# The second layer's expert stage: 32 more tokens gather the rows they chose, on four partitions each, and 352 instead of 384 go through all experts

## The chip, the cores and the metric

One core of a Trainium2 chip runs the whole program. The metric is device microseconds (us) from launch to the end, the median of several runs. TensorE (PE), VectorE (DVE), ScalarE (ACT), GpSimd (POOL) and SyncE (SP) work side by side. SP, ACT and POOL issue DMAs, which all run on the same 16 DMA engines.

## The reference

Two layers of a diffusion backbone over 512 latent tokens and 256 context tokens of width 1024. Each layer is a token mixer and then an expert stage, `peer_ffn`. In the second layer only the 512 latent tokens go through the expert stage. Of 16384 experts (128 x 128) every token chooses 128 (8 heads x 16), and its output is a weighted sum over these:

```python
q = (xb @ wq).reshape(T, 8, 2, 128)
s = einsum('thcq,hckq->thck', q, keys)
sv, si = top_k(s, 16)                       # per half of the key
top_s, top_j = top_k(sv[:,:,0,:,None] + sv[:,:,1,None,:], 16)
eidx = take(si[0]*128 + si[1], top_j)       # 128 experts of a token
gate = softmax(top_s)
act = gelu(einsum('td,thkd->thk', xb, u_tab[eidx]))
out = einsum('thk,thkd->td', gate * act, v_tab[eidx])
```

## The kernel before

`peer(l, xin)` is the expert stage of layer `l`. It treats its tokens in two ways at once.

**Dense tokens** (the first `Wd`: 512 of 768 in layer 0, 384 of 512 in layer 1) go through all 16384 experts, 128 of them at a time. `s_part(j)` loads 128 rows of U (`d.ur`, three buffers), splits them into a rounded part and a rest on ACT and DVE (`d.uh`, `d.ul`), and multiplies them with the activations in 24 matmuls (8 slices of the width x 3 products of the parts) whose moving side has `Wd` columns. ACT applies gelu and ACT's queue writes the result to DRAM (`Ad`). In the second loop over j ("V loop", `for j in range(NE)`) SP loads `Ad[j]`, 128 rows of V (`rt.vr`) and, every fourth j, a block of gates (`rt.gt` from `Gd`). DVE multiplies activation and gate (`rt.gm`), ACT and DVE split both V and the product, and PE adds 24 matmuls of `Wd` columns into eight PSUM banks.

The gates are built in between: `route` turns the scores of a tile of 128 tokens into expert numbers and gates on DVE. `build` takes `128 // GB` = 4 blocks of 32 tokens; a block makes one-hot tables on DVE, 64 fp16 matmuls on PE, and one 2 MB write to `Gd` from ACT's queue. `s_ahead(n)` puts n `s_part`s ahead of a route or a block, in layer 1 six before a route (twelve before the first) and three before a block. What is left of the 128 is done one by one in `trailing`.

**Gathered tokens** (the last 128 in layer 1, 256 in layer 0) sit one on each partition. For each of a token's 128 experts an indirect DMA of POOL (line 1524) fetches one row of U per partition into `grow` (128 x 1024 fp32, six buffers in layer 1, four in layer 0), and DVE takes the dot product with the token's row (line 1497). After gelu and gate, 128 more DMAs fetch rows of V, which DVE adds up (line 244, `tok`). `choose(n, after)` uses the gathers of two calls before, copies n indices (`at`) on DVE and issues n gathers. In layer 1 it is called with 3 twice per block, with 1 per `trailing` step, and in the V loop with `(NS - done) // max(1, CHE - j)`, `NS` = 256 and `CHE` = 128.

At the end all gathered sums are transposed on PE and added to x. The instructions of one engine are laid out by a list scheduler ahead of time, so the parts of a route stand between other DVE work, and engines run their own list in order.

Names in rows: `d.S` is the PSUM tile of `s_part`, `O` that of the V loop, `pv` the split parts of V and product, `rt.k` PSUM of routes and builds; a name's prefix (`rt.`, `d.`, `mrg.`) says only in which section the tile was made.

Of the kernel before, what the change touches and what calls it, by code (L numbers as in the profile page):

```python
# [11 lines left out]
F32, F32R, U32, I32, U8 = dt.float32, dt.float32r, dt.uint32, dt.int32, dt.uint8  # L12
# [195 lines left out]
NG = (2, 1)  # L208
TOK = (2, 1)
# [7 lines left out]
def body(tc, I, out, dbg=None, stop=None):  # L217
# [17 lines left out]
    def tt(o, a, b, op):  # L235
        return V.tensor_tensor(o, a, b, op=op)
# [41 lines left out]
    with pool("keep") as kp, pool("scr", space=DRAM) as dp:  # L278
# [1134 lines left out]
        def peer(l, xin):  # L1413
# [6 lines left out]
            Wd = W - 128 * NG[l]  # L1420
            NB = Wd // GB
            NS = 256 * NG[l]
# [15 lines left out]
            with pool("pnrm", side=far) as np_:  # L1438
                h = norm_mod((hp, hg), np_, psS, x, l, 1, t0, "S", Wd if CUT[l] else None)
# [35 lines left out]
            def token_rows(t):  # L1475

                r = T(gp, [128, 8, 128], F32, "grow", GBUF[l])
                a, _, hi, lo = h[-1]
# [12 lines left out]
            gs, got, done = [], [], [0, 0]  # L1491

            def use(g, r):
                s, e = gs[r // 256], r % 128
                w = s["w"]
                if r % 256 < 128:
                    V.scalar_tensor_tensor(g, g, 1.0, s["h"], A.mult, A.mult, accum_out=w[:, e:e + 1])  # L1497
                    if e == 127:
                        act(w, w, AF.Gelu_apprx_tanh)
                        tt(w, w, s["gate"], A.mult)  # L1500
                elif e == 0:
                    s["y"] = T(gp, [128, 1024], F32, "tok", TOK[l])
                    ts(s["y"], g, w[:, 0:1])
                else:
                    stt(s["y"], g, w[:, e:e + 1], s["y"])

            def choose(n, after):
                n = min(n, 256 * len(gs) - done[0])
                with tc.issue_after(after.ins):
                    done[1] += 1  # L1510
                    while got and got[0][2] <= done[1] - LAG[l]:
                        use(*got.pop(0)[:2])
                    if n:
                        at = T(gp, [128, 8], I32, "at", 3)
                        i = 0
                        while i < n:
                            r = done[0] + i
                            m = min(n - i, 128 - r % 128)
                            V.tensor_copy(at[:, i:i + m], gs[r // 256]["ei"][:, r % 128:r % 128 + m])  # L1519
                            i += m  # L1520
                for i in range(n):
                    r = done[0]
                    g = T(gp, [128, 1024], F32, "grow", GBUF[l])
                    G.indirect_dma_start(out=g, out_offset=None,  # L1524
                                         in_=I["Ur"] if r % 256 < 128 else I["V"].rearrange("l j i d -> (l j i) d"),
                                         in_offset=bass.IndirectOffsetOnAxis(ap=at[:, i:i + 1], axis=0))
                    got.append((g, r, done[1]))
                    done[0] += 1
# [85 lines left out]
            def route_rows(p, t, io16):  # L1614
                ij, gate = route(p, t, io16)
                ef = T(p, [128, 128], F32, "gr", 2)
                fl = [ij[:, c].rearrange("p h k -> p (h k)") for c in range(2)]
                ts(ef, fl[1], float(NE), float(l * NE * NE))
                ei = T(gp, [128, 128], I32, "ei", NG[l])
                tt(ei, ef, fl[0], A.add)  # L1620
                gs.append(dict(ei=ei, gate=gate.rearrange("p h k -> p (h k)"), h=rows[NT - 1 - t],
                               w=T(gp, [128, 128], F32, "gw", NG[l]), at=t))

            ND = Wd // 128
# [22 lines left out]
            else:  # L1647
# [3 lines left out]
                rows = [token_rows(t) for t in range(NT - 1, ND - 1, -1)]  # L1651
            rq.release()
            with pool("rg", side=far) as p:
# [9 lines left out]
                def build(t, f):  # L1663
# [11 lines left out]
                    for b in range(128 // GB):  # L1675
# [31 lines left out]
                order += range(ND)  # L1707
                for t in order:
# [4 lines left out]
                    ij, _ = route(p, t, io16)  # L1713
                    build(t, [ij[:, c].rearrange("p h k -> p (h k)") for c in range(3)])
# [65 lines left out]
            for s in gs:  # L1780
                tk = slice(t0 + 128 * s["at"], t0 + 128 * s["at"] + 128)
                for a in range(0, 8, 4):
                    ps = pso[nu % 8].rearrange("p (k t) -> p k t", t=128)
# [58 lines left out]
```

## Time and profile before

| | us |
|---|---|
| median of 3 runs (4926.05 to 4934.66) | 4933.41 |
| the profiled execution | 4910.86 |
| its span in the trace | 4909.1 |
| PE busy | 4506.6 (92%) |
| DVE busy | 3626.7 (74%) |
| mean DMA rate over the span | 238 GB/s |

The profiled execution is 22.55 us under the median and its span leaves 1.76 us around it. A busy time is the union of an engine's instructions; matmuls overlap their neighbours, so their own durations are longer than the distance from one to the next. The DMA share is the mean busy share of the 16 engines. Layer 1's expert stage is roughly the last quarter of the span, from 3560 us on.

### The profile page before, as it was taken

Reading aid. Unit: us, or ns where it says so; the run is one execution under the profiler, and the core shown is the slowest. Engines: PE = TensorE matmul, PEld = TensorE weight load, DVE = VectorE, ACT = ScalarE, POOL = GpSimd, SP = SyncE. Lnnn points to the kernel's source line nnn. Section 1 sums busy time; section 2 is a strip of 40 time slices with the busy share of each in tenths; the row PEclk is TensorE's granted clock in tenths of the full one; section 3 lists DMA queues with packets and bytes.
Section 4 is the critical chain, followed back from the end, with each engine's and each line's share of the span. In section 5 each row is a group of like instructions: output and inputs, shape, how many; then the busy total and the mean of one; then the engine's idle time right before and its main releaser. Section 6 shows DMA issues by size and latency. Waiting matters only on the chain. (4 is left out here: it accounts for less than half of the span.)

```text
span 4909.1 us, 66824 instructions
## 1 busy us (share of the span) xinstructions
PE 4506.6 (92%) x24203; PEld 3782.9 (77%) x24203; DVE 3626.7 (74%) x7303; ACT 1686.9 (34%) x2548; POOL 1358.9 (28%) x1117
## 2 busy tenths in 40 slices
PE   7879898899999999799999887998899998999998
PEld 4659576688777888687788664767589898999997
DVE  5772667499889997688898677466589975577787
ACT  4352223443223333222222435222533333333333
POOL 1211101002344544234555221111002332223332
PEclk9989998899999999899999998999999999999999
DMA  5441624356788999999999544334327889988896
GB/s 181 162 136 64 204 93 122 136 174 226 250 303 300 332 335 340 315 358 355 367 383 378 176 152 131 105 129 129 130 83 244 285 307 330 300 290 323 324 333 245
DMA packets 521083, 1170.01 MB, mean 238 GB/s; under 512 B 68192, under 2 KB 250272, under 8 KB 516272
## 3 DMA queue, kind: packets, MB, share of 16 engines
q1 hardware_dynamic: 227440, 563.42, 32.9%
q0 software_dynamic: 134912, 484.06, 27.8%
q10 hardware_dynamic: 158400, 118.25, 7.5%
q8 instruction: 191, 3.13, 0.3%
q14 instruction: 140, 1.15, 0.1%
HBM read 992.95 MB, written 173.02 MB: 238 GB/s over the span
## 5 line engine op out<-in xcount | busy, mean ns | idle before, releaser
L254 PE MATMUL d.S<-mrg.hhi,d.ul 128*128 128x512 f32 (+1 forms) x2048 | 767.0, 375 | 71.7 <-DVE d.ul L251 63.0
L1524 POOL DMA_INDIRECT d.grow<-in_V_dram,d.at x369 | 572.0, 1550 | 709.5 <-DVE d.at L1519 570.8
L254 PE MATMUL d.S<-mrg.hlo,d.uh 128*128 128x512 f32 (+1 forms) x2048 | 756.8, 370 | 0.1
L254 PE MATMUL d.S<-mrg.hhi,d.uh 128*128 128x512 f32 (+1 forms) x2048 | 754.7, 369 | 0.0
L254 PE MATMUL rt.O<-rt.pv,rt.pv 128*128 128x512 f32 (+1 forms) x2580 | 556.5, 365 | 39.7 <-DVE rt.pv L251 38.9
L254 PEld LDWEIGHTS rt.O<-rt.pv,rt.pv 128*128 128x128 f32 x2580 | 466.8, 188 | 105.7 <-issue 46.5
L254 PEld LDWEIGHTS d.S<-mrg.hhi,d.ul 128*128 128x128 f32 x2048 | 395.4, 193 | 126.1 <-DVE d.ul L251 76.6
L247 ACT ACTIVATE d.pa<-d.S 128x512 f32<-128x512 f32 (+1 forms) x256 | 139.7, 546 | 861.4 <-PE d.S L254 817.7
L251 DVE TENSOR_TENSOR d.ul<-d.ur,d.uh 128x1024 fp32r<-128x1024 f32 x256 | 312.3, 1221 | 157.7 <-ACT d.uh L250 151.9
L254 PEld LDWEIGHTS d.S<-mrg.hlo,d.uh 128*128 128x128 f32 x2048 | 394.8, 193 | 39.5 <-DVE mrg.hlo L251 0.9
L254 PEld LDWEIGHTS d.S<-mrg.hhi,d.uh 128*128 128x128 f32 x2048 | 393.3, 192 | 41.4
L1524 POOL DMA_INDIRECT d.grow<-in_Ur_dram,d.at x233 | 306.5, 1315 | 425.5 <-DVE d.at L1519 320.0
L1524 POOL DMA_INDIRECT rt.grow<-in_Ur_dram,rt.at x151 | 215.9, 1430 | 612.7 <-DVE rt.at L1519 566.8
L250 ACT CAST rt.pv<-rt.vr 128x1024 fp32r<-128x1024 f32 x172 | 181.2, 1053 | 580.7 <-PE d.O L254 260.8
L1497 DVE SCALAR_TENSOR_TENSOR d.grow<-d.grow,rt.tok 128x1024 f32<-128x1024 f32 x233 | 281.8, 1222 | 101.3 <-DMA d.grow<-in_Ur_dram,d.at 100.0
L244 DVE SCALAR_TENSOR_TENSOR d.tok<-d.grow,rt.gw,d.tok 128x1024 f32<-128x1024 f32 x245 | 314.3, 1283 | 50.5 <-DMA d.grow<-in_V_dram,d.at 50.0
L254 PE MATMUL d.O<-rt.pv,rt.pv 128*128 128x512 f32 (+1 forms) x1548 | 338.0, 362 | 0.0
L254 PEld LDWEIGHTS d.O<-rt.pv,rt.pv 128*128 128x128 f32 x1548 | 281.4, 188 | 30.1
L254 PE MATMUL rt.O<-d.pv,d.pv 128*128 128x512 f32 (+1 forms) x1260 | 272.2, 365 | 7.6 <-DVE d.pv L251 7.2
L250 ACT CAST d.uh<-d.ur 128x1024 fp32r<-128x1024 f32 x256 | 266.6, 1042 | 27.9 <-issue 9.0
L254 PEld LDWEIGHTS rt.O<-d.pv,d.pv 128*128 128x128 f32 x1260 | 228.4, 189 | 40.0 <-issue 10.9
L254 PE MATMUL z.z<-hhi,z.wlo 128*128 128x512 f32 (+1 forms) x656 | 236.1, 360 | 23.0 <-POOL z.wlo L251 16.2
(619 smaller groups left out, 9173.7 us busy)
## 6 DMA issues: line engine op xcount, KB each, us to landing
d.ur<-in_U_dram SPq DMA_DIRECT2D x256, 512.0 KB
rt.vr<-in_V_dram SPq DMA_DIRECT2D x256, 512.0 KB
ada.adaw<-in_ada_w_dram POOLq DMA_DIRECT2D x80, 512.0 KB
mrg.Ad<-d.pa ACTq DMA_DIRECT2D x128, 256.0 KB
rt.gt<-mrg.Gd SPq DMA_DIRECT2D x32, 1024.0 KB
rt.ga<-mrg.Ad SPq DMA_DIRECT2D x128, 256.0 KB
mrg.Gd<-ro.x ACTq DMA_DIRECT2D x14, 2048.0 KB
mrg.Gd<-rt.gst ACTq DMA_DIRECT2D x14, 2048.0 KB
```

Of the source, the lines that this page charges most:

```text
L244: return V.scalar_tensor_tensor(o, a, s, b, op0=op0, op1=op1)
L247: return S.activation(o, i, f, bias=bias, scale=scale)
L250: S.copy(hi, src)
L251: return (eng or V).tensor_tensor(lo, src, hi.bitcast(F32), op=A.subtract)
L254: PE.matmul(ps, l, r, start=start, stop=stop)
L1497: V.scalar_tensor_tensor(g, g, 1.0, s["h"], A.mult, A.mult, accum_out=w[:, e:e + 1])
L1524: G.indirect_dma_start(out=g, out_offset=None, in_=I["Ur"] if r % 256 < 128 else I["V"].rearrange("l j i d -> (l j i) d"), in_offset=bass. ...
```

## The change

`QP = (0, 4)` switches it on in layer 1 only. 32 of the 384 dense tokens (the last quarter of dense tile 2) become gathered tokens. Each sits on four partitions, 32 of its 128 experts on each, so 32 gathers of U and 32 of V serve all four quarters together. `Wd` falls from 384 to 352 and `NB`, the blocks of gates, from 12 to 11; `NS` rises from 256 to 320. `choose` now takes its rows from a list `plan` in the order the groups were routed: 128 U and 128 V of the first group, then 32 U and 32 V of the second.

Tile 2 is routed and built first of the three dense tiles, with three blocks instead of four. `token_rows` is called once more, for tile 2; its result is written to DRAM (`some`). `route_some` computes the expert numbers and issues 12 DMAs on SP's queue that put numbers, gates and token rows onto the four partition groups. At the end 8 matmuls with 32 columns add the four partial sums and transpose them, and 8 DVE instructions of 32 columns add them to x. The knobs for how many gathers go where (`CHN`, `CHT`, `CHE`, `GBUF`, `LAG`) stay. Layer 0 computes as before.

```diff
+QP = (0, 4)
...
-            Wd = W - 128 * NG[l]
+            Wh = W - 128 * NG[l]
+            nq = 128 // QP[l] if QP[l] else 0
+            Wd = Wh - nq
             NB = Wd // GB
-            NS = 256 * NG[l]
+            NS = 256 * NG[l] + (256 // QP[l] if QP[l] else 0)
...
             def token_rows(t):
...
-                ht = T(gp, [128, 1024], F32, "tok", TOK[l])
+                ht = T(gp, [128, 1024], F32, "tok", TOK[l]) if t >= ND else T(gp, [128, 1024], F32, "grow", GBUF[l])
...
+            plan = []
+
+            def chosen(s):
+                gs.append(s)
+                plan.extend((s, i, e) for i in range(2) for e in range(s["n"]))
...
             def choose(n, after):
-                n = min(n, 256 * len(gs) - done[0])
+                n = min(n, len(plan) - done[0])
...
+            def route_some(p, ij):
+
+                n = QP[l]
+                ea = T(p, [128, 128], I32, "ea", 1)
+                numbers(p, ij, ea)
+                eq = T(gp, [128, nq], I32, "eq", 1)
+                gq = T(gp, [128, nq], F32, "gq", 1)
+                hq = T(gp, [128, 1024], F32, "tokq", 1)
+                gf = ij[:, 2].rearrange("p h k -> p (h k)")
+                m = 128 // n
+                for i in range(n):
+                    to, of = slice(nq * i, nq * i + nq), slice(m * i, m * i + m)
+                    SP.dma_start(eq[to], ea[128 - nq:, of])
+                    SP.dma_start(gq[to], gf[128 - nq:, of])
+                    SP.dma_start(hq[to], some[128 - nq:])
+                chosen(dict(ei=eq, gate=gq, h=hq, n=m, w=T(gp, [128, m], F32, "wq", 1), at=Wd, tag=("tokq", 1)))
...
                 rows = [token_rows(t) for t in range(NT - 1, ND - 1, -1)]
+                if nq:
+                    sm_ = token_rows(ND - 1)
+                    some = T(dp, [128, 1024], F32, "some%d" % l)
+                    SP.dma_start(some, sm_)
...
-                    for b in range(128 // GB):
+                    for b in range((Wd - 128 * t) // GB if t == ND - 1 else 128 // GB):
...
-                order += range(ND)
+                order += ([ND - 1] + list(range(ND - 1))) if nq else range(ND)
...
                     ij, _ = route(p, t, io16)
+                    if nq and t == ND - 1:
+                        route_some(p, ij)
...
+                if nt < 128:
+
+                    one = T(p, [128, nt], F32, "one")
+                    tt(one, ident[:, 0:nt], ident[:, nt:2 * nt], A.add)
+                    for i in range(2, QP[l]):
+                        tt(one, one, ident[:, nt * i:nt * i + nt], A.add)
...
-                        tr(ps[:, k - a], s["y"][:, 128 * k:128 * k + 128])
+                        if nt < 128:
+                            mm(ps[:, k - a], s["y"][:, 128 * k:128 * k + 128], one, True, True)
+                        else:
+                            tr(ps[:, k - a], s["y"][:, 128 * k:128 * k + 128])
```

## Rows read from the trace of the kernel before

**Rows 1.** Page, busy time, share of the span and instructions of each engine
```profile
PE 4506.6 (92%) x24203; PEld 3782.9 (77%) x24203; DVE 3626.7 (74%) x7303; ACT 1686.9 (34%) x2548; POOL 1358.9 (28%) x1117
```

**Rows 2.** Windows, layer 1's expert stage by stage: routes, builds, turn, trailing, V loop, end
```profile
core 0: us, PE busy (x) PEld busy (x) DVE busy (x) ACT busy (x) POOL busy (x), PEclk, DMA share, GB/s
3628.00:3740.00 112.00, 102.06 (x534) 95.41 (x533) 103.71 (x416) 40.93 (x60) 4.31 (x3) 0.95 0.35 114
3740.00:4050.00 310.00, 293.38 (x1866) 285.18 (x1865) 260.68 (x391) 122.41 (x195) 115.17 (x72) 0.96 0.90 305
4050.00:4083.00 33.00, 18.89 (x97) 18.25 (x96) 14.79 (x25) 8.69 (x13) 3.53 (x3) 0.84 0.94 338
4083.00:4329.00 246.00, 243.51 (x1391) 242.13 (x1390) 145.04 (x233) 83.16 (x118) 65.38 (x58) 0.99 0.89 305
4329.00:4883.00 554.00, 542.60 (x3052) 529.59 (x3052) 433.35 (x618) 184.21 (x251) 195.53 (x122) 1.00 0.87 316
...
4883.00:4909.00 26.00, 12.05 (x46) 6.72 (x44) 12.02 (x24) 8.81 (x12) 0.00 (x0) 0.79 0.21 81
```

**Rows 3.** Timeline, PE: start, us, line, names, shape; 23 steps of 256, then 8 of 384
```profile
2861.63 0.28 PE L254 MATMUL z.z<-hhi,z.wlo 128*128 128x256 f32 x1
...
2864.38 0.28 PE L254 MATMUL z.z<-hhi,z.whi 128*128 128x256 f32 x1
...
4249.79 0.33 PE L254 MATMUL d.S<-mrg.hhi,d.ul 128*128 128x384 f32 x1
...
4251.18 0.33 PE L254 MATMUL d.S<-mrg.hhi,d.uh 128*128 128x384 f32 x1
```

**Rows 4.** Waits, 4329 to 4872 (V loop): who waited for whom, us, times, longest
```profile
DVE rt.tok L244 <- DMA d.grow<-in_V_dram,d.at: 97.8, 79, 3.7
ACT rt.pv L250 <- DMA rt.vr<-in_V_dram: 73.2, 21, 5.1
...
ACT d.pv L250 <- DMA rt.vr<-in_V_dram: 44.5, 13, 5.6
```

**Rows 5.** DMA issues of the whole span: names, queue, count, KB each
```profile
rt.vr<-in_V_dram SPq DMA_DIRECT2D x256, 512.0 KB
...
mrg.Ad<-d.pa ACTq DMA_DIRECT2D x128, 192.0 KB
rt.gt<-mrg.Gd SPq DMA_DIRECT2D x32, 768.0 KB
rt.ga<-mrg.Ad SPq DMA_DIRECT2D x128, 192.0 KB
```

**Rows 6.** Windows, part of layer 0's V loop, then most of layer 1's
```profile
2400.00:2700.00 300.00, 298.99 (x1307) 244.31 (x1307) 270.17 (x325) 84.92 (x109) 160.35 (x109) 1.00 1.00 382
...
4450.00:4860.00 410.00, 399.62 (x2231) 387.21 (x2230) 322.57 (x463) 137.15 (x187) 154.43 (x93) 1.00 0.90 326
```

**Rows 7.** Groups on DVE: layer 0, 2400 to 2700; then layer 1, 4400 to 4850
```profile
L244 DVE SCALAR_TENSOR_TENSOR d.tok<-d.grow,rt.gw,d.tok 128x1024 f32<-128x1024 f32 x109 | 139.9, 1283 | 28.6 <-DMA d.grow<-in_V_dram,d.at 28.4
...
L236 DVE TENSOR_TENSOR rt.gm<-rt.ga,rt.gt 128x512 f32<-128x512 f32 x54 | 37.4, 692 | 1.9
...
L236 DVE TENSOR_TENSOR rt.gm<-rt.ga,rt.gt 128x384 f32<-128x384 f32 x101 | 56.4, 558 | 3.5
```

**Rows 8.** Timeline, the writes of one tile's four blocks on ACT's queue
```profile
3750.34 0.38 ACTq L1698 DMA_DIRECT2D mrg.Gd<-ro.x  x1
3770.58 0.38 ACTq L1698 DMA_DIRECT2D mrg.Gd<-rt.gst  x1
3793.85 0.38 ACTq L1698 DMA_DIRECT2D mrg.Gd<-ro.x  x1
3814.96 0.38 ACTq L1698 DMA_DIRECT2D mrg.Gd<-rt.gst  x1
```

**Rows 9.** Waits of SP's queue, 3740 to 4330
```profile
SPq L1762 <- DMA mrg.Gd<-rt.gst: 13.3, 1, 13.3
```

**Rows 10.** Timeline: SP's load of U, the transposes of a token tile
```profile
4029.79 0.33 SPq L1450 DMA_DIRECT2D d.ur<-in_U_dram  x1
...
3650.07 1.04 PE L264 MATMUL rt.k<-cst,rt.grow 128*128 128x128 f32 x8
```

**Rows 11.** Groups on PE, 3740 to 4050 (builds)
```profile
L254 PE MATMUL d.S<-mrg.hhi,d.ul 128*128 128x384 f32 x364 | 129.3, 355 | 8.1 <-DVE d.ul L251 8.1
...
L254 PE MATMUL rt.k<-rt.og,ro.x 128*128 128x128 f16 x768 | 97.1, 297 | 8.6 <-ACT rt.gst L247 5.3 <-ACT ro.x L247 3.3
```

**Rows 12.** Timeline, DVE: the last additions to x
```profile
4883.06 2.72 DVE L244 SCALAR_TENSOR_TENSOR ro.x<-rt.O,mods,ro.x 128x384 f32<-128x384 f32 x5 [2.08 <-PE rt.O L254]
...
4887.26 2.15 DVE L244 SCALAR_TENSOR_TENSOR ro.x<-rt.O,mods,ro.x 128x128 f32<-128x128 f32 x8
```

More of the change, by code (lines that the diff above doesn't have):

```diff
@@ L1438, in peer @@
             with pool("pnrm", side=far) as np_:
-                h = norm_mod((hp, hg), np_, psS, x, l, 1, t0, "S", Wd if CUT[l] else None)
+                h = norm_mod((hp, hg), np_, psS, x, l, 1, t0, "S", Wh if CUT[l] else None)
             hi, lo = h[0][2:]
@@ L1477, in token_rows @@
                 r = T(gp, [128, 8, 128], F32, "grow", GBUF[l])
-                a, _, hi, lo = h[-1]
+                a, _, hi, lo = h[-1] if t >= ND else h[0]
                 tk = slice(128 * t - a, 128 * t - a + 128)
                 tt(r, hi[:, :, tk].bitcast(F32), lo[:, :, tk].bitcast(F32), A.add)
-                ht = T(gp, [128, 1024], F32, "tok", TOK[l])
+                ht = T(gp, [128, 1024], F32, "tok", TOK[l]) if t >= ND else T(gp, [128, 1024], F32, "grow", GBUF[l])
                 for a in range(0, 8, 4):
@@ L1491, in peer @@
             gs, got, done = [], [], [0, 0]
+            plan = []
+            def chosen(s):
+                gs.append(s)
+                plan.extend((s, i, e) for i in range(2) for e in range(s["n"]))
             def use(g, r):
-                s, e = gs[r // 256], r % 128
+                s, second, e = plan[r]
                 w = s["w"]
-                if r % 256 < 128:
+                if not second:
                     V.scalar_tensor_tensor(g, g, 1.0, s["h"], A.mult, A.mult, accum_out=w[:, e:e + 1])
-                    if e == 127:
+                    if e == s["n"] - 1:
                         act(w, w, AF.Gelu_apprx_tanh)
@@ L1516, in choose @@
                         while i < n:
[L1517 to L1519 removed]
+                            s, _, e = plan[done[0] + i]
+                            m = min(n - i, s["n"] - e)
+                            V.tensor_copy(at[:, i:i + m], s["ei"][:, e:e + m])
                             i += m
@@ L1524, in choose @@
                     G.indirect_dma_start(out=g, out_offset=None,
-                                         in_=I["Ur"] if r % 256 < 128 else I["V"].rearrange("l j i d -> (l j i) d"),
+                                         in_=I["V"].rearrange("l j i d -> (l j i) d") if plan[r][1] else I["Ur"],
                                          in_offset=bass.IndirectOffsetOnAxis(ap=at[:, i:i + 1], axis=0))
@@ L1612, in route, with numbers @@
                 return ij, gate
-            def route_rows(p, t, io16):
-                ij, gate = route(p, t, io16)
+            def numbers(p, ij, ei):
                 ef = T(p, [128, 128], F32, "gr", 2)
@@ L1618, in route_rows @@
                 ts(ef, fl[1], float(NE), float(l * NE * NE))
+                tt(ei, ef, fl[0], A.add)
+            def route_rows(p, t, io16):
+                ij, gate = route(p, t, io16)
                 ei = T(gp, [128, 128], I32, "ei", NG[l])
[L1620 to L1624, printed above, removed]
+                numbers(p, ij, ei)
+                chosen(dict(ei=ei, gate=gate.rearrange("p h k -> p (h k)"), h=rows[NT - 1 - t], n=128,
+                            w=T(gp, [128, 128], F32, "gw", NG[l]), at=128 * t, tag=("tok", TOK[l])))
+            def route_some(p, ij):
[13 more added lines that the diff above has]
+                chosen(dict(ei=eq, gate=gq, h=hq, n=m, w=T(gp, [128, m], F32, "wq", 1), at=Wd, tag=("tokq", 1)))
+            ND = Wh // 128
             SP.dma_start(xs[:, :, t0:], x[:, :, t0:])
@@ L1780, in peer @@
             for s in gs:
-                tk = slice(t0 + 128 * s["at"], t0 + 128 * s["at"] + 128)
+                nt = 128 if s["n"] == 128 else nq
+                tk = slice(t0 + s["at"], t0 + s["at"] + nt)
+                if nt < 128:
[3 more added lines that the diff above has]
+                        tt(one, one, ident[:, nt * i:nt * i + nt], A.add)
                 for a in range(0, 8, 4):
-                    ps = pso[nu % 8].rearrange("p (k t) -> p k t", t=128)
+                    ps = pso[nu % 8][:, 0:4 * nt].rearrange("p (k t) -> p k t", t=nt)
                     nu += 1
                     for k in range(a, a + 4):
-                        tr(ps[:, k - a], s["y"][:, 128 * k:128 * k + 128])
+                        if nt < 128:
+                            mm(ps[:, k - a], s["y"][:, 128 * k:128 * k + 128], one, True, True)
+                        else:
+                            tr(ps[:, k - a], s["y"][:, 128 * k:128 * k + 128])
                     for k in range(a, a + 4):
```

2 lines of the change are left out of this document (1 added, 1 removed).

## Prediction

> **What bounds the kernel now.** I start with the page's busy times [rows 1]: PE leads with 92% of the span, but that is a mean over many stages, and only layer 1's expert stage changes. So the windows come next, stage by stage [rows 2]. The reader should see three regimes. In *trailing* (4083 to 4329) PE is busy 243.5 of 246 us and the DMA share is 0.89: PE is the bound. In the *builds* (3740 to 4050) PE has 293 of 310, DVE 261 and the DMAs 0.90: three resources close together. In the *V loop* (4329 to 4883) PE shows 543 of 554, but it is not quite the limit. The matmul pitch says so [rows 3]: eight steps of 384 columns take 1.39 us, 0.174 each, so the 24 of one expert row j need 4.17 us, while 554 / 128 is 4.33. The waits name what is late [rows 4]: DVE waits 79 times, 97.8 us, for a gather to land, and ACT 73.2 + 44.5 us for a load of V. The V loop is a PE loop that leans on the DMAs.
>
> **The traffic per j in the V loop.** From the issue sizes [rows 5]: V 512 KB, `Ad` 192 KB, a quarter of 768 KB of gates, and one gather of 128 x 1024 fp32, 512 KB: 1408 KB now. After the change `Ad` and the gates shrink by 1/12 to 176 KB each: 1376 KB with one gather, 1888 KB with two.
>
> **How the gathers are spread.** This is arithmetic on the code, and it decides the case. Before: 12 blocks x 6 = 72 gathers in the builds, 62 in trailing (66 of the 128 U steps are placed with routes and builds), 122 left: none for the first six j, then one per j. After: 11 x 6 = 66, then 65 in trailing (63 U steps are placed earlier), 189 left for 128 j. The integer division gives 1 per j up to j = 66 and 2 per j for the last 61. So all the new gathers, and more, pile up in the last half of the V loop.
>
> **The change part by part.** All of it is against the profiled execution.
>
> *Narrower matmuls.* The pitch is 2.75 / 23 = 0.1196 us at 256 columns and 0.174 at 384 [rows 3], 0.42 ns a column, so 352 columns give 0.160: 3.85 us per j and stage instead of 4.17, 0.325 saved. Over 256 such steps that is 83 us, if nothing else is late. The rest of the sum is how much of that survives.
>
> *Routes (3628 to 3740).* 427 `d.S` matmuls run here, 17.8 steps; DVE, with the routes, is busy 104 of 112, as much as PE [rows 2]. 17.8 x 0.325 = 5.8 is the most; I take -4, ends 0 and -6.
>
> *Builds.* Within one tile the blocks' writes are 20.2, 23.3 and 21.1 us apart [rows 8], so a block is worth 21.5 us, and one goes: -21.5. The other 45 or so U steps here (364 x 3 / 24 [rows 11]) less three would save 42.5 x 0.325 = 13.8 on PE, but the 64 fp16 matmuls per block (768 for 12) do not shrink, and neither do DVE's tables or the gathers per block. I take half, -6.5. Sum -28, ends -21 and -35. The order of tiles (2, 0, 1) costs nothing: the same work in another order; its cover is the six U steps before each route.
>
> *The turn (4050 to 4083).* PE is busy 19 of 33 while the last gate write and the reload of x drain. They stay: 0.
>
> *Trailing.* 62 steps at 4.17 become 65. The DMAs carry 512 + 512 + 176 = 1200 KB per step; over 3.85 us that is 319 GB/s, against 305 at a share of 0.89 now [rows 2], so about 0.93. I allow 3.9 us: 253.5 - 258.5 = -5. Ends -8 (3.85) and +12 (no narrowing gain at all, three steps more).
>
> *V loop, first 67 j (one gather).* PE wants 3.85. The DMAs deliver 326 GB/s now [rows 6], which gives 1409 KB (in thousands) / 326 = 4.32, no gain. Between these ends I take 4.2, nearer to the row of the same loop, since the gather and V waits of rows 4 don't get shorter with fewer columns.
>
> *V loop, last 61 j (two gathers).* No such stretch exists in layer 1, but layer 0's V loop is one [rows 6]: 109 gathers on 54 j [rows 7], two per j. There the DMA share is 1.00 at 382 GB/s, and a j takes 300 / 54.5 = 5.5 us, where PE at 512 columns needs just as long (299 of 300 busy). Here PE would need 3.85, and DVE's busy time, 270 / 54.5 = 4.96, less twice 0.692 - 0.525 for the narrower product and its split (0.558 at 384 columns, 0.525 at 352 by the same slope), is 4.6. The DMAs need 1933 KB / 382 = 5.06. So the DMAs are last, 5.06 at best; layer 0's 5.5 is the other end. I take 5.2, near the first, because layer 0's 5.5 is PE's own need there.
> Here a page of the Trainium skill speaks otherwise: "DMA: Bandwidth & Descriptors", section "Where 436 GB/s comes from", puts the fabric ceiling at 435 GB/s and the HBM share of a core at about 358. By the first a j would be an estimated 4.4 us, by the second 5.4. No 300 us here show more than 382, which is above the one and below the other.
>
> V loop: 67 x 4.2 + 61 x 5.2 = 598.6 against 554, +45. Ends: 67 x 3.85 + 61 x 5.06 = 566.6, +13; 67 x 4.33 + 61 x 5.5 = 625.6, +72.
>
> *Added steps.* The extra `token_rows` is 8 transposes, 1.04 us on PE [rows 10], two copies, an addition and one 512 KB write: +2, ends 0 and 3. `route_some` puts 12 DMAs on SP's queue, 0.33 us each by the load of U [rows 10], 4 us of issue, and they wait for tile 2's route on DVE. Queued behind them are the loads of U; for these waits ACT's `d.uh`, then `d.ul`, then PE. With three U buffers loaded ahead most is hidden; if the list scheduler puts them before the route has finished, SP stands as it does now for a gate write, 13.3 us [rows 9]. I take +4, ends 0 and 13. At the end, four gathers instead of two are still to be added after the last j, plus 8 small matmuls and 8 DVE instructions (8 of 128 columns take 2.15 us [rows 12]): +4, ends 0 and 6. The new group's DVE and POOL work in the middle is inside the 5.2.
>
> **Sum.** -4 - 28 + 0 - 5 + 45 + 2 + 4 + 4 = +18. On the profiled 4910.86 that is 4929. The median of the three runs is 22.55 us above the profiled one; I carry that over unchanged: 4933.4 + 18 = 4951, 0.36% slower. About 0.2%, 10 us, is what a measurement can tell from no change.
>
> **The rivals.**
> *The queue absorbs it (faster).* Layer 0 runs full queues without losing PE time. If the same holds here, the first 67 j run at PE's 3.85 and the others at 5.06, +13; with builds at -34, trailing -7, routes -5 and added steps +6 the sum is -27: 4906. For it: share 1.00 at 382 GB/s in rows 6. Against: at one gather per j layer 1 has only 0.90 of share and waits all the same [rows 4]. It decides whether the first 67 j fall below about 4.0 us.
> *The gather chain (slower still).* DVE adds a row two calls after its issue, and a V split stands behind that wait in DVE's list. Two gathers per call make the landing later. Then the first half stays at 4.33 and the second is at layer 0's 5.5: +72 in place of +45, 4978. For it: 97.8 us of such waits already [rows 4]. Against: in layer 0 DVE waits only 28.6 us in 300 with two gathers and four buffers [rows 7].
> *Narrowing is worth nothing on PE.* Weight loads are busy 242 of 246 us in trailing [rows 2]. If they set the pitch, U steps and the first half stay as they are: routes 0, builds -21, trailing +12, V loop 67 x 4.33 + 61 x 5.2, +53, added +10: +54, 4987. Against it: at 256 columns the same kind of matmul, each with its own 128 x 128 weights, starts every 0.12 us [rows 3], which a load of 0.17 could not follow. The Trainium skill, "Perfetto Trace Analysis", section "Identifying the Most-Contended Engine", takes the weight-load busy share as the measure of TensorE's headroom; the pitch at 256 columns disagrees with reading it so here.
>
> **How the numbers follow.** My forecast 0.47, the absorbing queue 0.20, the gather chain 0.20, weight loads 0.05, and 0.08 that gains and losses cancel near zero. The range from 4908 to 4988 takes in most of the first rival and all of the second, and the forecast's unknowns; about 2 in 10 stay outside. The forecast itself spreads by some 20 us, so it gives part of its chance to no change. Faster by over 0.2%: 0.22; within 0.2%: 0.22; slower: 0.56.
>
> **What would show it.** Right: in the windows of the changed kernel the trailing stage shows about 3.9 us per step; the V loop is about 600 us long, with two stretches, the first near 4.2 us per j, the second near 5.2 with a DMA share near 1.00, 370 to 385 GB/s, and PE well below 90%; and one block fewer, some 28 us, before the turn. Wrong: a second half at 4.6 or less (then the DMAs deliver over 420 GB/s), a first half under 4.0, or trailing still at 4.17. A new wait of SP over 10 us in the builds would show `route_some` dearer than I put it.

## The result and the profile after

The changed kernel takes 4963.91 us (4958.61 to 4973.0, five runs), the one before 4933.41 in the same comparison: a ratio of 1.0075, 95% interval 1.0057 to 1.0093, 0.75% slower. The forecast was 4951 with a range from 4908 to 4988. The direction and the largest term came out, and the size within a factor of two (18 us slower forecast, 30.5 measured); the terms of trailing and of the end didn't, and the reason given for the first half of the V loop was wrong.

The page of the changed kernel, busy times (answers rows 1):

```profile
PE 4461.7 (90%) x24163; PEld 3724.8 (75%) x24163; DVE 3679.7 (74%) x7413; ACT 1678.7 (34%) x2543; POOL 1452.2 (29%) x1181
```

PE has 45 us less to do than before and the kernel is still slower: PE's work is not what was saved or lost. The windows of the changed kernel, columns as in rows 2: routes, builds, most of trailing, V loop with one gather, V loop with two, end:

```profile
3542.00:3742.00 200.00, 192.63 (x1032) 169.31 (x1031) 179.54 (x799) 76.84 (x125) 6.58 (x2) 0.99 0.34 109
3742.00:4036.70 294.70, 258.18 (x1711) 250.87 (x1711) 248.81 (x405) 113.59 (x182) 109.16 (x66) 0.90 0.87 288
4090.00:4300.00 210.00, 202.88 (x1221) 197.20 (x1221) 123.91 (x202) 71.47 (x102) 73.37 (x50) 0.99 0.90 308
4325.00:4610.00 285.00, 264.99 (x1563) 254.69 (x1562) 221.71 (x323) 94.13 (x130) 107.15 (x66) 0.98 0.89 317
4610.00:4925.00 315.00, 265.12 (x1501) 254.87 (x1500) 273.06 (x399) 90.82 (x122) 164.43 (x122) 0.95 0.98 365
4925.00:4961.00 36.00, 14.76 (x45) 8.25 (x44) 16.91 (x34) 8.80 (x12) 0.00 (x0) 0.74 0.23 87
```

Compare with rows 2. The second half of the V loop is the new thing: DMA share 0.98 at 365 GB/s, PE 265 of 315 us. The line above it looks like the old V loop, but PE there is busy 93%, not 98%. In the builds PE fell to 258 of 295, with a mean granted clock of 0.90 (before 0.96; the clock's levels are 1.2 and 2.4 GHz).

So that stages of different kernels can be set side by side, they are cut at events of the timeline: the starts of the first `d.S` matmul, of the first and the last fp16 matmul of the builds and of the last `d.S`, the end of the last `O` matmul, the end of the span. (Some expectations below cut the builds at the start of the last unbroken row of fp16 matmuls, which comes 1 to 3 us earlier.) All stages in us:

| kernel | routes | builds | U rest | V loop | end | sum | first `d.S` at |
|---|---|---|---|---|---|---|---|
| before | 213.7 | 308.1 | 279.6 | 558.0 | 22.4 | 1381.9 | 3527.2 |
| before, a second trace | 214.0 | 306.0 | 279.6 | 560.2 | 22.5 | 1382.2 | 3539.9 |
| the change | 199.2 | 295.6 | 285.9 | 602.3 | 35.6 | 1418.6 | 3542.7 |
| narrow_only | 197.0 | 292.9 | 282.1 | 556.8 | 22.5 | 1351.3 | 3530.0 |
| gathers_only | 215.3 | 301.6 | 286.9 | 604.8 | 35.4 | 1444.0 | 3549.2 |
| block_less | 211.4 | 290.2 | 291.6 | 559.1 | 22.4 | 1374.7 | 3535.2 |
| order_only | 215.4 | 309.8 | 280.3 | 564.1 | 22.4 | 1392.0 | 3543.1 |
| lag3 | 201.6 | 291.8 | 286.3 | 543.6 | 37.0 | 1360.4 | 3542.0 |
| before_lag3 | 211.9 | 310.9 | 281.5 | 532.8 | 22.4 | 1359.4 | 3531.9 |
| even_lag3 | 201.4 | 298.9 | 284.8 | 527.6 | 31.7 | 1344.4 | 3538.4 |
| trail3 | 200.4 | 296.3 | 269.1 | 526.8 | 30.9 | 1323.6 | 3534.5 |

The change costs 36.7 us by this table, 30.5 by the medians. The spans differ by 52, but 15.5 of that lies ahead of the first `d.S`, where nothing was changed.

Who waits in the two halves of the V loop of the changed kernel (waits on DVE, ACT and PE: total us, times, longest; the first three lines are of 4325 to 4610, the others of 4610 to 4925):

```profile
DVE rt.tok L246 <- DMA d.grow<-in_V_dram,d.at: 60.9, 47, 3.8
ACT rt.pv L252 <- DMA rt.vr<-in_V_dram: 69.1, 20, 6.0
PE rt.O L256 <- DVE rt.pv L253: 15.6, 15, 2.3
...
DVE rt.tok L246 <- DMA d.grow<-in_V_dram,d.at: 20.7, 19, 3.2
DVE d.grow L1506 <- DMA d.grow<-in_Ur_dram,d.at: 15.9, 15, 2.9
ACT rt.pv L252 <- DMA rt.vr<-in_V_dram: 38.9, 17, 6.4
```

The old wait of rows 4 is still there in the first half: DVE waits for a gather 47 times in about 66 rounds.

### The profile page after: what moved, and what is told of

Same layout as the page of the kernel before. It is cut to its first block, busy times and chain, and to the rows that moved or that the text cites. A ratio compares the mean times of both kernels' runs of the same rounds, so it can differ in the third digit from the quotient of the medians.

```text
span 4961.3 us, 66925 instructions
## 1 busy us (share of the span) xinstructions
PE 4461.7 (90%) x24163; PEld 3724.8 (75%) x24163; DVE 3679.7 (74%) x7413; ACT 1678.7 (34%) x2543; POOL 1452.2 (29%) x1181
## 3 DMA queue, kind: packets, MB, share of 16 engines
q14 instruction: 142, 1.16, 0.1%
## 5 line engine op out<-in xcount | busy, mean ns | idle before, releaser
L256 PE MATMUL d.S<-mrg.hhi,d.ul 128*128 128x512 f32 (+1 forms) x2048 | 756.5, 369 | 76.5 <-DVE d.ul L253 67.5
L1533 POOL DMA_INDIRECT d.grow<-in_V_dram,d.at x404 | 611.8, 1514 | 638.3 <-DVE d.at L1528 480.3
L256 PE MATMUL d.S<-mrg.hlo,d.uh 128*128 128x512 f32 (+1 forms) x2048 | 744.6, 364 | 0.1
L256 PE MATMUL d.S<-mrg.hhi,d.uh 128*128 128x512 f32 (+1 forms) x2048 | 741.0, 362 | 0.0
L256 PE MATMUL rt.O<-rt.pv,rt.pv 128*128 128x512 f32 (+1 forms) x2580 | 560.2, 367 | 83.5 <-DVE rt.pv L253 70.0
L1533 POOL DMA_INDIRECT d.grow<-in_Ur_dram,d.at x265 | 338.0, 1276 | 478.0 <-DVE d.at L1528 367.0
L1533 POOL DMA_INDIRECT rt.grow<-in_Ur_dram,rt.at x151 | 237.4, 1572 | 592.1 <-DVE rt.at L1528 548.2
L256 PE MATMUL rt.O<-d.pv,d.pv 128*128 128x512 f32 (+1 forms) x1260 | 267.6, 361 | 23.4 <-DVE d.pv L253 16.9
```

The source lines that it names most:

```text
L256: PE.matmul(ps, l, r, start=start, stop=stop)
L1533: G.indirect_dma_start(out=g, out_offset=None, in_=I["V"].rearrange("l j i d -> (l j i) d") if plan[r][1] else I["Ur"], in_offset=bass.Ind ...
```

## Experiments

The comparisons of one group share their runs of the kernel before, so its median differs a little from group to group (4925.71, 4925.25, 4930.56).

### The two halves of the change, each alone

narrow_only, against the changed kernel:

```diff
-            NS = 256 * NG[l] + (256 // QP[l] if QP[l] else 0)
+            NS = 256 * NG[l]
...
-                if nq:
-                    sm_ = token_rows(ND - 1)
...
-                    if nq and t == ND - 1:
-                        route_some(p, ij)
```

> The changed kernel without the second group of gathered tokens: 352 dense tokens, 256 gathers as in the kernel before, and no expert output for 32 tokens. It is the narrowing alone. If the pitch of a matmul follows its columns (24 in 3.85 us instead of 4.17), trailing runs at 3.9 us a step and the V loop at about 4.2 us per j, 538 us in place of 558 before and 602 after; the end loses its 13 us again: about 4885 us, 1% faster than the kernel before. If the weight loads set the pitch, trailing and V loop stay at 4.17 and 4.33 and only the missing block is gained: about 4923.

Measured: 4895.11 us, ratio 0.9942 (0.9925 to 0.996), 30.6 us faster. But the V loop is 556.8, as long as at 384 columns, where 538 was expected. Its waits on DVE and ACT, 4302 to 4859:

```profile
4302.00:4859.00 557.00, 517.41 (x3079) 497.32 (x3078) 431.77 (x630) 181.72 (x251) 202.62 (x124) 0.99 0.86 311
...
DVE rt.tok L246 <- DMA d.grow<-in_V_dram,d.at: 112.7, 89, 3.8
ACT rt.pv L252 <- DMA rt.vr<-in_V_dram: 114.1, 31, 5.8
```

gathers_only, against the changed kernel:

```diff
-            Wd = Wh - nq
+            Wd = Wh
...
-                chosen(dict(ei=eq, gate=gq, h=hq, n=m, w=T(gp, [128, m], F32, "wq", 1), at=Wd, tag=("tokq", 1)))
+                chosen(dict(ei=eq, gate=gq, h=hq, n=m, w=T(gp, [128, m], F32, "wq", 1), at=Wh - nq, tag=("tokq", 1)))
```

> The changed kernel with 384 dense tokens and 12 blocks of gates, and the second group gathered on top (32 tokens get their expert output twice). It is the cost of the 64 gathers alone. If the DMAs are full in the last 61 j (1920 KB per j at 382 GB/s is 5.15 us), the V loop is 67 x 4.33 + 61 x 5.15 = 604 us against 558 before, and the end takes 13 us more: about 4990 us, 1.2% slower than before. If two gathers per j fit beside 24 matmuls of 384 columns (the loop stays near 4.4), it is the end alone: about 4950.

Measured: 4989.66, ratio 1.0123 (1.0106 to 1.014), 64 us slower. The halves add up: 64 - 30.6 = 33, the change within its interval. What the 32 tokens save as dense tokens lies outside the V loop; of the 62.1 us that they cost as gathered ones by the table, 46.8 lie in it and 13.0 in the end.

### Is it bytes or the spread: even and half_bytes

even spreads the 189 gathers over all 128 j:

```diff
+                if j == 0:
+                    left = NS - done[0], done[0]
+                share = left[1] + left[0] * (j + 1) // NE - done[0] if l else (NS - done[0]) // max(1, CHE - j)
-                choose(min(8, (NS - done[0]) // max(1, CHE - j)), ins)
+                choose(min(8, share), ins)
```

> The changed kernel with the 189 gathers of the V loop spread evenly, 1 or 2 per j by the running sum, in place of 1 per j for 67 j and 2 per j for 61. Nothing else changes. If the loss comes from full DMAs in the second half alone, a j carries 1620 KB, 4.34 us at 382 GB/s, and the V loop falls from 602 to between 560 and 580: some 30 us faster than the changed kernel, about 4933. If every gather costs its share wherever it stands (4.2 with one, 5.2 with two, 4.7 in the mean), the loop stays at 602 and the time at 4964.

Measured: 5045.15, ratio 1.0251 (1.0227 to 1.0276): far slower, where both expectations had it no slower than the changed kernel. The V loop takes 678 us at only 305 GB/s. First its window, then the timeline of DVE (even, 4650 to 4668):

```profile
4325.00:5003.00 678.00, 569.50 (x3073) 538.99 (x3071) 497.85 (x723) 186.31 (x252) 217.46 (x188) 0.91 0.88 305
...
4652.32 0.14 DVE L1528 COPY d.at<-rt.ei 128x1 int32<-128x1 int32 x1
...
4656.43 1.28 DVE L246 SCALAR_TENSOR_TENSOR rt.tok<-d.grow,rt.gw,rt.tok 128x1024 f32<-128x1024 f32 x1 [3.47 <-DMA d.grow<-in_V_dram,d.at]
...
4660.68 0.15 DVE L1528 COPY d.at<-rt.ei 128x1 int32<-128x1 int32 x1
...
4663.94 0.16 DVE L1528 COPY d.at<-rt.ei 128x2 int32<-128x2 int32 x1
```

From copy to copy these two rounds take 8.4 and 3.3 us; over the loop, rounds that begin with the copy of one number take 5.8 us in the mean and those that begin with two 4.9. So bytes alone don't set this loop: in its second half fewer bytes per j made it slower. The long round shown copies one number, but it ends behind a pair that was copied at 4649.0, two rounds before. Why the alternation is dearer than the two old stretches together was not taken apart; with three rounds to land in the loop falls to 527.6 us (even_lag3, below).

half_bytes leaves the spread as it is, and lets the gathers from number 198 on (counted from 0), those of the last 61 j, fetch 512 numbers instead of 1024. DVE reads these twice, so its work stays:

```diff
...
+                    part_ = l == 1 and r >= 198
+                    G.indirect_dma_start(out=g[:, 0:512] if part_ else g, out_offset=None,
+                                         in_=tab.rearrange("r (h c) -> (r h) c", c=512) if part_ else tab,
...
```

> The changed kernel in which the gathers from the 198th on (those of the last 61 j) fetch 512 numbers of a row instead of 1024, and DVE reads that half twice, so that DVE, POOL and the number of DMAs stay and only the bytes fall (what these gathers add to the output is wrong). A j carries 1376 KB as in the first half. If the bytes set the second half's 5.16 us, it falls to DVE's own pace, 4.5 to 4.6: 61 x 0.6 = 37 us faster than the changed kernel, about 4927. If POOL's issue or the wait for two landings sets it, it stays at 5.1 and the time within 10 us of 4964.

Measured: 4931.25, ratio 1.001 (0.9998 to 1.0021). The second half of the V loop in the windows:

```profile
4618.00:4897.00 279.00, 253.99 (x1494) 241.42 (x1493) 270.30 (x400) 89.88 (x121) 191.68 (x122) 0.99 0.87 299
```

DVE's products (`rt.gm`, one per j) are 4.63 us apart here, 5.23 in the changed kernel, and DVE is busy 270 of 279: close to DVE's own pace, which the prediction had put at 4.6. So in the second half of the changed kernel it is the landing of 512 KB gathers that is late, not DVE's work.

### The lag of two calls: lag3, before_lag3, even_lag3, trail3

`choose` uses a row two calls after it asked for it. lag3 makes it three, in layer 1's V loop alone:

```diff
-            gs, got, done = [], [], [0, 0]
+            gs, got, done, lag = [], [], [0, 0], [LAG[l]]
...
-                    while got and got[0][2] <= done[1] - LAG[l]:
+                    while got and got[0][2] <= done[1] - lag[0]:
...
+            lag[0] += l
             for j in range(NE):
```

> The changed kernel in which layer 1's V loop uses a gathered row three calls after its issue instead of two (six buffers still suffice). If the first half's 4.35 us per j is the wait for gathers in DVE's order, it falls to about 3.9 and the second half, full of bytes, stays at 5.1: about 25 us faster than the changed kernel, 4939. If the first half is held by the loads of V or by the DMA rate, nothing changes: 4964.

Measured: 4903.13, ratio 0.9951 (0.9932 to 0.997): 61 us off the changed kernel, where 25 were expected; the changed kernel is then faster than before. The second half, which was expected to stay, fell as well. Windows of the two halves:

```profile
4322.00:4567.00 245.00, 245.00 (x1531) 245.00 (x1530) 218.45 (x320) 90.89 (x127) 67.89 (x66) 1.00 0.98 366
...
4567.00:4865.00 298.00, 267.67 (x1544) 259.22 (x1543) 273.53 (x404) 90.98 (x125) 168.21 (x122) 0.94 1.01 391
```

The first half runs at PE's pace, without a gap: 1531 / 24 = 63.8 j in 245 us, 3.84 each. The mechanism is to be read in two timelines. The changed kernel, DVE and POOL from 4451 to 4460:

```profile
4451.16 1.28 DVE L246 SCALAR_TENSOR_TENSOR rt.tok<-d.grow,rt.gw,rt.tok 128x1024 f32<-128x1024 f32 x1 [1.44 <-DMA d.grow<-in_V_dram,d.at]
...
4452.36 0.15 DVE L1528 COPY d.at<-rt.ei 128x1 int32<-128x1 int32 x1
4452.42 1.22 DVE L253 TENSOR_TENSOR rt.pv<-rt.vr,rt.pv 128x1024 fp32r<-128x1024 f32 x1
4452.77 1.68 POOL L1533 DMA_INDIRECT d.grow<-in_V_dram,d.at  x1 [3.23 <-DVE d.at L1528]
...
4456.12 1.28 DVE L246 SCALAR_TENSOR_TENSOR rt.tok<-d.grow,rt.gw,rt.tok 128x1024 f32<-128x1024 f32 x1 [1.48 <-DMA d.grow<-in_V_dram,d.at]
...
4459.76 1.28 DVE L246 SCALAR_TENSOR_TENSOR rt.tok<-d.grow,rt.gw,rt.tok 128x1024 f32<-128x1024 f32 x1 [0.17 <-DMA d.grow<-in_V_dram,d.at]
```

The numbers copied at 4452.36 belong to the row that is added at 4459.76: 7.4 us from copy to landing. Then 1.2 us of addition, and only then the next copy. Two rounds hold 7.4 + 1.2 = 8.6, so a round can't be shorter than 4.3, whatever PE needs; DVE's split of V (at 4452.42) stands behind the same wait, and PE behind that split. In lag3 the same lines carry no wait and stand 3.85 apart:

```profile
4452.25 1.28 DVE L246 SCALAR_TENSOR_TENSOR rt.tok<-d.grow,rt.gw,rt.tok 128x1024 f32<-128x1024 f32 x1
...
4453.45 0.14 DVE L1528 COPY d.at<-rt.ei 128x1 int32<-128x1 int32 x1
...
4453.86 0.94 POOL L1533 DMA_INDIRECT d.grow<-in_V_dram,d.at  x1 [2.92 <-DVE d.at L1528]
...
4456.10 1.28 DVE L246 SCALAR_TENSOR_TENSOR rt.tok<-d.grow,rt.gw,rt.tok 128x1024 f32<-128x1024 f32 x1
```

before_lag3 is the control, the same edit in the kernel before.

> The kernel before with the third call of lag in layer 1's V loop. Its loop takes 4.36 us per j where 24 matmuls need 4.17. If the wait for gathers is the difference, the loop falls from 558 to about 538 us: 0.4% faster than the kernel before, about 4907. If the loads of V are, it stays at 4926.

Measured: 4896.15, ratio 0.9944 (0.9926 to 0.9961). The V loop falls to 532.8 us, 4.16 per j, which is 24 matmuls of 384 columns at their own pitch [rows 3], and PE is busy throughout:

```profile
4336.00:4869.00 533.00, 533.00 (x3077) 532.97 (x3076) 438.95 (x625) 183.25 (x251) 114.99 (x122) 1.00 0.91 329
```

So the kernel before was held by the lag already, by 25 us; the change pays at the lag where it should have paid at PE. With the lag out of the way the change is about even, 4903 against 4896. In the V loop, between DVE's products, its first half wins 0.3 us per j (3.84 against 4.16) and its second loses 0.7 (4.85 against 4.16).

even_lag3 joins both edits. With three rounds to land in, spreading should no longer hurt.

> The evenly spread kernel (5045 us) with the same third call of lag. If its 5.3 us per j came from gathers that had only a short call to land in, the loop falls to 4.4 to 4.6 us per j, the rate of 1620 KB at 360 to 380 GB/s: 565 to 590 us in place of 678, about 4940. If alternating one and two gathers disturbs the loads of V themselves, it stays above 5.0 and the time above 5000.

Measured: 4874.62, ratio 0.9897 (0.988 to 0.9914), the V loop 527.6 us, shorter than the 565 to 590 expected. PE (97%) and the DMAs are both close to full now:

```profile
4324.00:4851.00 527.00, 512.57 (x3071) 495.61 (x3069) 493.41 (x722) 179.99 (x252) 210.81 (x188) 0.99 1.01 392
```

trail3 begins with the lag of three calls in `trailing` (from its second step; at the first the six buffers are still held by the builds).

```diff
                         choose(CHT[l], last[0])
+                        lag[0] = LAG[l] + l
...
-            lag[0] += l
```

> The kernel even_lag3 with the three-call lag from the second trailing step on, instead of from the V loop on. In the changed kernel a trailing step takes 4.08 us, although 24 matmuls of 352 columns need 3.86, and DVE stands 69.3 us in 210 for the landing of a gather of U. Theory A (the two-call lag sets the trailing pace, as it set the V loop's): about 58 steps fall to 3.86 to 3.9 us, 10 to 13 us less from the last build matmul to the last d.S, total about 4863 (4858 to 4868). Rival B (the loads of U and the 0.89 DMA share set the pace): the wait moves to d.ur, nothing gained, 4875.

Measured: 4866.74, ratio 0.9881 (0.9857 to 0.9905), the fastest of all. The rest of U falls from 284.8 to 269.1 us, more than theory A asked. Trailing with two calls of lag in the changed kernel, then with three in trail3, 4090 to 4290:

```profile
4090.00:4290.00 200.00, 193.04 (x1163) 187.93 (x1163) 118.06 (x193) 68.21 (x98) 70.03 (x48) 0.99 0.90 309
DVE rt.grow L1506 <- DMA rt.grow<-in_Ur_dram,rt.at: 63.3, 37, 3.9
```

```profile
4090.00:4290.00 200.00, 200.00 (x1252) 200.00 (x1251) 126.65 (x208) 73.12 (x105) 49.09 (x53) 1.00 0.93 327
```

1163 matmuls are 48.5 steps of 4.13 us, 1252 are 52.2 of 3.83. The wait did not move to the loads of U: PE is busy for all of the 200 us. Rival B falls.

### Where the gain of the builds went: gd_on_sp, block_less, order_only, before_again

The builds became only 11.5 us shorter (295.6 against 307.1, the mean of two traces). A first suspicion came from ACT's queue. The timeline of the changed kernel, issues on ACT's queue:

```profile
3891.47 0.38 ACTq L1731 DMA_DIRECT2D mrg.Gd<-ro.x  x1
3895.18 10.24 ACTq L1473 DMA_DIRECT2D mrg.Ad<-d.pa  x1
3906.01 0.33 ACTq L1473 DMA_DIRECT2D mrg.Ad<-d.pa  x1
```

A small write that usually takes 0.33 us to issue was held 10.24 behind a 2 MB gate write. Over the builds all issues on ACT's queue sum to 70.8 us, and nine of them that take over 1 us make up 55.6; before the change the sums are 35.8 and 18.0. gd_on_sp lets SP issue the gate writes.

```diff
-                        S.dma_start(Gd[:, :, t * (128 // GB) + b]...
+                        (SP if l else S).dma_start(Gd[:, :, t * (128 // GB) + b]...
```

> The changed kernel with layer 1's 2 MB gate writes issued from SP's queue instead of ACT's. In the changed kernel the issue of the next Ad write on ACT's queue, 3.7 us behind a gate write, is held for 3.4 to 10.2 us (11 times, 71 us in all, against 35 before), and PSUM evacuations wait behind it. If that holds the builds up, these issues fall to 0.33 us and the builds shrink from 295 to about 280 us: 10 to 15 us faster than the changed kernel, about 4950. If the builds are held by the DMAs or by DVE, they stay at 295 and the time at 4964; if SP's loads of U are now held instead, they grow.

Measured: 4958.56, ratio 1.0064 (1.004 to 1.0087). The held issues are gone and the builds stay at 296.2: the theory fell. Other waits took their place; ACT now stands for the loads of U, whose queue the gate writes hold:

```profile
ACT d.uh L252 <- DMA d.ur<-in_U_dram: 61.7, 13, 8.9
```

block_less takes one gate block out of the kernel before, and nothing else.

```diff
-                    for b in range(128 // GB):
+                    for b in range(128 // GB - (l if t == ND - 1 else 0)):
...
-                    SP.dma_start(gt, Gd[j // GJ, :, :NB])
+                    SP.dma_start(gt[:, :NB - l], Gd[j // GJ, :, :NB - l])
+                    if l:
+                        SP.dma_start(gt[:, NB - 1], Gd[j // GJ, :, 0])
```

> The kernel before, with 384 dense tokens and its gathers, but the last 32 dense tokens get no gate block of their own (the V loop reads block 0 twice in its place, so their output is other than the reference's). It prices the block that the change removes. Its three U steps move into trailing, 12.5 us. Theory A (a block is worth the 21.5 us between two writes, as forecast): builds 21.5 shorter, from the first build matmul to the last d.S 9 shorter, total about 4917. Then of the 13 us that narrow_only gained there, 4 are left for the narrower matmuls, of 28 forecast. Rival B (the narrower matmuls do gain in the builds and the block is worth less, about 14 us between writes): nothing gained from the first build matmul to the last d.S, total about 4926.

Measured: 4916.87, ratio 0.9967 (0.9943 to 0.9992). Against the mean of before's two traces the routes are 2.5 us shorter, the builds 16.9 (290.2 against 307.1), and the rest of U is 12.0 longer; the stages together lose 7.3, all of it ahead of the V loop. Theory A, near enough.

order_only is the kernel before with `order += [ND - 1] + list(range(ND - 1)) if l else range(ND)`.

> The kernel before with its dense tiles routed and built in the order 2, 0, 1, nothing else. The change's order was costed at 0. Theory A (order is free): each stage within 2 us, total within 0.2% of before, about 4925. Rival B (in that order the tables and the U steps stand worse, which would be where the missing gain of the builds went): builds 10 to 15 us longer than the 306 us of the first trace, total about 4938.

Measured: 4926.51, ratio 0.9996 (0.998 to 1.0011). The total says that order is free. In its one trace the builds are 2.7 us and the V loop 5 longer than the mean of before's two, past the 2 us that theory A allowed; with one trace I can't say whether that is the order.

before_again is the unchanged kernel, for a second trace.

> The unchanged kernel before, for a second trace of it. Its profiled execution took 4910.86, its other runs about 4925. Theory A: the difference lies in the stages before layer 1's expert stage, and the stages compared here (builds 306, last build matmul to last d.S 282, V loop 558, tail 22) stay within 3 us each. Rival B: it lies in layer 1's V loop, where the gather wait has slack of its own, 5 to 15 us longer, and then the gap of 44 us between the two V loops was read too large.

Measured: one run, 4923.95, 13.1 us over the first profiled one. Its stages agree with the first trace within 2.2 us each, and its first `d.S` comes 12.8 us later: theory A. So these 13 us between two runs of one kernel lie ahead of the stage that was changed.

block_less and narrow_only have the same blocks and the same steps, so their difference is the narrowing alone (with the order of tiles, which order_only prices): routes 14.4 us less, builds 2.7 more, rest of U 9.5 less, V loop 2.4 less. Routes and builds go together here: a list scheduler lays out DVE's work, and what of a route isn't done when the first build starts is done in the builds. Their windows show it (block_less, then narrow_only; routes, then builds):

```profile
3535.20:3746.60 211.40, 201.00 (x1022) 176.24 (x1021) 186.61 (x837) 78.75 (x125) 3.69 (x3) 0.98 0.31 100
3746.60:4036.80 290.20, 272.53 (x1719) 265.21 (x1719) 241.15 (x366) 112.93 (x179) 107.82 (x66) 0.94 0.88 296
...
3530.00:3727.00 197.00, 191.68 (x1022) 169.29 (x1021) 174.49 (x774) 75.06 (x122) 6.68 (x2) 0.99 0.32 105
3727.00:4020.00 293.00, 256.52 (x1720) 248.49 (x1719) 253.34 (x430) 114.17 (x183) 108.84 (x67) 0.91 0.88 291
```

DVE's busy time over both stages is 427.8 us in either kernel; 12.1 of it moved from the routes to the builds. Together the stages gain 11.7. Why not more is to be read on DVE's waits in the builds of narrow_only (3727 to 4019, 292.0 us, DVE busy 252.6):

```profile
3727.00:4019.00 292.00, 255.57 (x1711) 247.53 (x1711) 252.58 (x430) 113.20 (x182) 108.84 (x67) 0.91 0.88 290
...
PE rt.k L256 <- ACT rt.gst L249: 23.9, 10, 4.1
...
DVE d.ul L253 <- ACT d.uh L252: 37.4, 14, 6.2
```

DVE's work and this one wait are 290 of the 292 us, so DVE has no other slack, and PE, with less to do, waits instead: 23.9 us for the evacuation `rt.gst` against 5.3 [rows 11]. That the wait for `d.uh` comes from ACT working through its own list in order is my reading; it wasn't tried.

## Why the prediction came out as it did

| term | forecast | measured | from |
|---|---|---|---|
| block removed, with its three steps in trailing | -21.5 + 12.5 = -9 | -8.3 | block_less - before, up to the V loop |
| narrowing in routes and builds | -4 - 6.5 = -10.5 | -11.7 | narrow_only - block_less |
| narrowing in trailing | -17.5 | -9.5 | the same |
| added steps ahead of the V loop | +6 | +8.8 | change - narrow_only |
| V loop, both causes | +45 | +44.3 | change - before |
| end | +4 | +13.1 | change - before |
| sum | +18 | +36.7 | |

The forecast's -5 for trailing is split here into the three steps more (+12.5) and 65 steps at 0.27 less (-17.5). Before stands with its first trace; with the mean of its two, the block is -7.4 and the V loop +43.3.

**The V loop** came out in its sum and in its second half: from the first round with two gathers (j = 67, counted from 0) to the end it takes 319.3 us, its products 5.23 apart, where 5.2 was forecast at 370 to 385 GB/s; 365 were measured. That the sum fits so closely is in part luck: the first half was 0.2 us per j dearer than forecast, and the forecast counted from a window of 554 us, where the events give 558. Its reason was half right. "DMAs last" was written as a matter of bytes at 382 GB/s. lag3 moves the same bytes in 298 us at 391, so 365 was no limit: what was late is the landing of a pair of gathers two rounds after it was asked for, which depends on its bytes (half_bytes) and on the rounds it is given (lag3). With three rounds the DMA share there is 1.01, and 1933 KB / 391 is 4.9 us, near the 4.85 between its products: once the lag is out of the way the bytes do set this half, so the forecast's floor of 5.06 was nearly right and the lag is the rest. The Trainium skill, "DMA: Bandwidth & Descriptors", section "Where 436 GB/s comes from", gives a core's HBM share as about 358 GB/s and the fabric's ceiling as 435. The 392 GB/s that even_lag3 holds for 527 us is above the first, so the first didn't bind here, and below the second.

**The step that failed in the first half** is "between these ends I take 4.2, nearer to the row of the same loop". It should have been that row itself, 4.33: between the products of j = 5 and j = 67 a j took 4.39 (the products before these are made ahead). The prediction weighed PE's 3.85 against a mean rate of the DMAs, 326 GB/s, but a rate that is reached while everyone waits is a result, not a limit. The right row was already there, DVE's 79 waits for a gather [rows 4], read with the code: a row used two calls after its issue means that two rounds can't be shorter than copy, issue, landing and addition. The gather chain was listed as a rival and its mechanism holds for this half; only its price for the second half, layer 0's 5.5, was too high.

**Trailing** failed for the same reason. 3.9 per step was forecast from PE and bytes, 4.13 measured, and the prediction itself had named "trailing still at 4.17" as its refutation. Before, the loop ran at PE's 4.17 and PE itself hardly waited, but the trace held a sign that the prediction did not read, DVE's waits in trailing (before, 4083 to 4329):

```profile
DVE rt.grow L1497 <- DMA rt.grow<-in_Ur_dram,rt.at: 30.9, 16, 4.7
```

So the lag was nearly as long as PE's step already. The narrower matmul uncovered it: DVE waits 63.3 us in 200. trail3 shows it by taking it away.

**The end** was sized by instructions (+4) and not by who stands in whose way. After the last `O` matmul DVE has four gathered rows left, and its list mixes them with the additions to x (timeline of DVE, changed kernel):

```profile
4927.78 1.27 DVE L246 SCALAR_TENSOR_TENSOR d.tokq<-d.grow,rt.wq,d.tokq 128x1024 f32<-128x1024 f32 x1
4928.97 0.34 DVE L246 SCALAR_TENSOR_TENSOR ro.x<-rt.O,mods,ro.x 128x128 f32<-128x128 f32 x1
...
4932.14 1.27 DVE L246 SCALAR_TENSOR_TENSOR d.tokq<-d.grow,rt.wq,d.tokq 128x1024 f32<-128x1024 f32 x1
...
4937.13 0.72 DVE L246 SCALAR_TENSOR_TENSOR ro.x<-rt.O,mods,ro.x 128x32 f32<-128x32 f32 x4 [0.98 <-PE rt.O L256]
```

The last addition ends 12.1 us after the last `O` matmul (4925.8 to 4937.9), before 2.7 [rows 12]. That is 9.3 of the 13.1; the other 4 lie after the last addition, in the final norm, and why stays open.

**Right, and for the reason given:** a block's price from the distance of its writes (16.9 of 21.5, and with its steps in trailing 8.3 of 9); SP's `route_some` (it issues ahead of the builds, and the longest wait of SP there, 22.9 us, stands in narrow_only too, which has no `route_some`); the order of tiles, by the total (0.9996); the gain of routes and builds taken together (11.7 against 10.5), as the work of DVE in them, 427.8 us, did not shrink. The rival that weight loads set the pitch falls with lag3's 3.84 us per j. In trail3's row above, weight loads are busy 200.00 of 200.00 us at 3.83 per step, and before the change 242.13 of 246 at 4.17 [rows 2]. The Trainium skill, "Perfetto Trace Analysis", section "Identifying the Most-Contended Engine", takes that busy share as a measure of TensorE's headroom; here it was full at both widths, so it could not tell that fewer columns would shorten the step.

**The median.** The forecast carried the 22.55 us between profile and median over unchanged. The changed kernel's profiled run lies only 0.8 us under its median, so the two spans differ by 52 us where the medians differ by 30.5; 15.5 of the 52 lie ahead of the first `d.S` and are not the change's.

## What to carry to other kernels

Where an engine uses a gather a fixed number of rounds after asking for it, work out copy to landing, plus the use, divided by that number: that is a floor of the round, and if it lies near the current pace, making the busiest engine's work smaller buys nothing. A DMA rate read from a loop that waits for its own DMAs is no limit; look for a stretch where they are never waited for in turn, or lengthen the lag by one. The same change was 0.75% slower with a lag of two calls, and with a lag of three and an even spread it is part of a kernel 1.2% faster than the one it started from. Not all of that is the change's: the lag of three in the V loop alone makes the old kernel 0.6% faster (before_lag3), and the old kernel with three calls in trailing too was not run.

## What the runs showed of the hardware that was not expected

- An issue of a small write on ACT's queue took up to 10.24 us when it came 3.7 us after a 2 MB write of 512-byte pieces on the same queue, 0.33 mostly. With the 2 MB writes on SP's queue (gd_on_sp) no issue on ACT's took over 1 us in the builds.
- An indirect DMA's instruction on POOL was held while DVE split V. In the V loop of the kernel before, 111 of 122 started in the midst of such a split; 108 of these took 1.67 us or nearly, and 110 ended 0.81 us after the split did. In before_lag3, the same kernel with the lag of three, none did, and 121 of 122 took 0.94. It isn't the waiting for gathers as such: in even, whose V loop is the longest, they took 1.16 in the mean. In the timelines above, the 1.68 at 4452.77 against lag3's 0.94 is some 0.7 of the 7.4 us from copy to landing, so part of what the lag costs. No run moved the split alone.
- Routes gained 14.4 us by narrowing where 21 steps at 0.325 explain 6.8. The 12.1 us of DVE's work that moved from the routes to the builds are the likely rest. The mean granted clock in the routes rose from 0.98 (block_less) to 0.99 (narrow_only), while in the builds, where PE now waits, it fell from 0.94 to 0.91; how much of either time is the clock's stays open.
